# The pooled branch and the merge gates of the second block, computed inside its attention and parked in DRAM

## The chip, the cores and the metric

The kernel runs on one core of one Trainium2 chip. The time is device microseconds of that core, from one launch of the whole program; the time given is the median of several executions.

## The reference

Two transformer blocks are applied to 512 tokens of 1024 features, in float32. The first has latent attention beside a retention branch, and a layer of 16,384 experts. The change lies in the mixer of the second block:

```python
h = rms_norm(x, norm_mix)
u, q, kc, vc, ksl, vsl, kwn, vwn, g_nsa, g_merge = split(h @ w_in)
y_pool = pool_mixer(u, w_pool, pool_scale)   # means over the last 2, 4, 8, 16 tokens less the token, times w_pool
y_nsa = nsa_mixer(q, kc, ..., g_nsa)         # 16 heads, 2 groups: compressed, selected and window keys
g_a, g_b = split(sigmoid(g_merge))
merged = g_a * (y_pool @ w_proj_pool) + g_b * (y_nsa @ w_proj_nsa)
x = x + merged @ w_out
```

After it come a norm, a feed-forward layer of 4096 hidden features, and the last norm. `y_pool`, `g_a` and `g_b` need `h` alone; only `y_nsa @ w_proj_nsa` needs the attention.

## The kernel before

**Arithmetic.** Arrays are kept as [feature, token]: tiles of 128 features on the partitions and 512 tokens along them. A product in float32 is made of three passes over operands that are split into a high and a low part (`hi` is the value rounded to float32r, `lo` the rest). `fm` (L249) multiplies 128 columns of a weight with all 512 tokens: 24 matmuls of 512 columns where the input has 1024 features (3 passes of 8 tiles), 12 where it has 512. `weights` loads one chunk of weights by a DMA on SyncE's queue (L222, 512 KB for 1024 features), rounds it on ScalarE (L210, tile `wh`) and subtracts on VectorE or GpSimd (L211, tile `wl`); the engine of the subtraction alternates from chunk to chunk. There are two buffers each for the raw chunk, `wh` and `wl`.

**The second block's mixer**, in the order of the code. The normed input `hn` (tiles `h2h`, `h2l` in the profile) is made; the keys and values of the three kinds follow. Then for each of two groups `g`: `queries(g)` makes the group's queries (four chunks `w_q`, each rotated in `rope_fm`, which passes it through a DMA on ScalarE's queue), and `attend(i, g, c, ...)` is called for four tiles `i` of 128 queries and two sets `c` of four heads, eight times a group. One `attend` makes the scores (PE, L1401 and L1402), adds the mask and takes the maximum (VectorE, L1431), the exponential (ScalarE, L1436), the compressed keys' softmax (`cs`, with GpSimd at L1441, L1444, L1449), scales by gate over sum (L1457 on VectorE, L1455 on GpSimd for one head of four), transposes (PE, L1469, copied out at L1471) and multiplies with the values (PE, L1474, into the one PSUM bank of the kind `o`). The result is split into `ynh` and `ynl`.

After both groups come the pooled branch (four chunks `w_u`, shifted sums on VectorE and GpSimd, L1491 to L1507; a product with `w_pool`, L1516, into `yps`) and the merge: for each of eight chunks `c` of 128 output features a gate `y` (`gate`, weights `w_gm`), the attention's projection (`gated`, `w_pn`, 24 matmuls), a gate `x` (`w_gm`), the pooled projection (`w_pp`, 12 matmuls), and `merged`, which adds the two:

```python
def gate(name, c, x):
    w = wfm(name, c)
    ps = mmps()
    fm(ps, w, hn, 0, 0, T)
    S.activation(x, ps, AF.Tanh, scale=0.5)
    return x
...
    V.scalar_tensor_tensor(x, x, 1.0, ps, op0=OP.add, op1=OP.mult)
...
for c in range(KD):
    y = gate("w_gm", KD + c, two(t2)[:, :T])
    gated("w_pn", c, ysl, KD, y)
    x = gate("w_gm", c, two(t2)[:, :T])
    gated("w_pp", c, yp, 4, x)
    merged(x, y, mg, c)
```

`residual` then multiplies with `w_out2` and adds to the residual stream `h1`, which stays in SBUF all the while, in the two halves of the kind `xb`.

**Who sets the order.** Here the instructions are not placed by hand. A scheduler orders them when the program is compiled: each engine, and SyncE's queue of DMAs, gets one fixed order, in which the instructions that come first in the code go first among those that the scheduler holds to be ready. On the chip each engine runs its own order strictly. Tiles are handed out from pools: the kind `t2` of this block has five buffers of 2 KB a partition (queries' rotation, shifted sums and gates share it), PSUM has two banks of the kind `mm`, which all products with weights share.

Of the kernel before, what the change touches and what calls it, by code (L numbers as in the profile page):

```python
# [9 lines left out]
F32 = mybir.dt.float32  # L10
# [8 lines left out]
T = 512          # tokens whose outputs are wanted  # L19
M = 16           # meta tokens; in the key order they come after the tokens  # L20
# [31 lines left out]
def _constants():  # L52
# [5 lines left out]
    tri01 = (q[None, :] >= q[:, None]).astype(f)                       # [m, c]  # L58
# [47 lines left out]
def _layout(i):  # L106
    i = {k: np.asarray(v) for k, v in i.items()}
    a = _constants()
    h = np.concatenate([i["x"][0], i["meta_tokens"]], 0)               # [528, 1024]
# [36 lines left out]
    pe = np.stack([i["pe_k_2"][0], i["pe_v_2"][0]], 0)                  # [2, 32, 64]  # L146
    pe = pe.transpose(2, 0, 1).reshape(64, 64)
    a["pe"] = np.ascontiguousarray(np.concatenate([pe, pe], 0))          # [(g dh), (k/v, l)]
    a["w_c1"] = np.stack([i[n][0].reshape(2, 16, 64, 256).transpose(0, 2, 1, 3).reshape(P, 16 * 256)  # half, dh, l, hidden
# [16 lines left out]
# ---------------------------------------------------------------- the program  # L166
def build(tc, A, OUT):
# [29 lines left out]
    # constants  # L197
# [10 lines left out]
    def split(src, hi, lo, lo_eng=None):  # L208
        """hi is src rounded to float32r, lo the rest."""
        S.copy(hi, src)  # L210
        (lo_eng or V).tensor_tensor(lo, src, hi.bitcast(F32), op=OP.subtract)  # L211
# [6 lines left out]
    def weights(ap, n, lo_pool=3, tag="w"):  # L218
        """One chunk of weights from DRAM, split in two float32r parts."""
# [14 lines left out]
    def wfm(name, c, kt=KD, width=P, c0=0):  # L234
        """some columns of weights, by tiles of features"""
        n = kt * width
        return kview(weights(A[name][c][:, c0:c0 + n], n, 2), kt, width)
# [7 lines left out]
    def fm(out, w, act, c0, t0, n, kt=KD, hooks=()):  # L245
        """out [128 columns of w, n tokens]; hooks: what comes after the first, the second pass"""
# [7 lines left out]
    def tm(out, w, act, c0, n, t0, m, kt=KD):  # L254
        """out [m tokens, n columns of w]"""
# [8 lines left out]
    def rstd_cols(sqs, n, width, out, first=0, after=None):  # L264
        """out[token, tile] = 1 / sqrt(mean over the features + eps) of the tokens from first up to n; sqs(t0, m):
        the squares of m tokens, [feature, token]; after: a factor of the tokens that comes first, and into out."""
# [17 lines left out]
    def ks(t):  # L284
        """the tiles [128, tokens] of t [128, k, tokens]"""
        return [t[:, k] for k in range(t.shape[1])]
# [3 lines left out]
    class Squares:  # L290
        """sum of the squares of the tiles [128 features, n tokens] of the residual stream, as they come"""
# [3 lines left out]
        def add(self, x, eng=None, a=0, b=None, last=False):  # L295
            """the last tile's squares stay by themselves"""
# [12 lines left out]
    class Norm:  # L309
        """RMS norm over the features (partitions and tiles) of the tiles src, some tokens after the others;  # L310
        put(k, tile, a, b): tokens a .. b of a normed tile."""
        def __init__(self, src, sqs, g0, put, pieces=HALVES, dst=None):
# [3 lines left out]
            S.activation(self.col[:, 7:8], eps, AF.Sqrt)    # (its table is in place when the norm needs it)  # L316
            self.rowt = two(sqs.tp, "row")

        def cols(self, i):
            """1 / sqrt(mean + eps) of each token"""  # L320
# [3 lines left out]
        def row(self, i):  # L324
            """the same, along the partitions"""
# [31 lines left out]
    def by_halves(act, jobs, hooks=()):  # L357
        """products of act with columns of weights, jobs: (weights, first column, done(ps, a, b)); all jobs for
        half of the tokens, then for the other; hooks: what comes within the first product"""
# [7 lines left out]
    def residual(get, act, sqs=None, norm=None):  # L367
        """adds act's product with the weights get(k) (and their first column) to the residual stream; the last
        tiles by halves of the tokens, with the first half's norm among the products of the second"""
# [20 lines left out]
    def rope_op(dst, src, c, sn, sp, shape, tp, add=None):  # L390
        """dst = rotation of src, both [m, heads, 2 * half]; c, sn, sp: cos, -sin, sin"""
# [15 lines left out]
    def rope_tab(rope, off, w, m, h):  # L407
        """views of a packed table [cos | cos | -sin | sin], the same for each head"""
# [9 lines left out]
    def two(tp, name="t2", dt=F32):  # L418
        """a tile of 2 KB a partition, of a kind shared by many short lives"""
        return tp.tile([P, L], dt, name=name, tag="t2")  # L420

    # halves of arrays [feature, token]: the residual stream, and the experts' inputs
# [6 lines left out]
    hd = dp.tile([KD, P, T], F32, name="hd")                # the residual stream, while the experts run  # L429
# [3 lines left out]
    # ================================================================ first block: mixer  # L433
# [24 lines left out]
    # the latents come from the tokens before their norm, which goes into the latents' own: y = h gain / rms(h), and  # L458
    # rms of a latent c of y is sqrt(r^2 mean(c'^2) + eps), r = 1 / rms(h), c' = the latent of h gain
# [20 lines left out]
    # latent queries and keys, [feature, token], gained but not yet normed  # L480
# [27 lines left out]
    # shared rotary key, [token, 32]  # L508
# [25 lines left out]
    # four heads at a time: queries [96, head, token], their norm in the scale of the scores; keys  # L534
    # [96, head, (meta, token)]; values [token, head, 64]
# [4 lines left out]
    # the values of the meta tokens, one block of rows and columns per head  # L540
# [66 lines left out]
    # ---- retention: the decay since the start of the sequence is in the rotations' tables  # L607
    xh, qz = halves("rq", "xa")                             # queries of a head, zeros for the pair's other head
# [3 lines left out]
    kf = half_slot("rkf")                                   # keys [two heads' 64, pair, token]  # L612
    ktm = half_slot("rkt")[:, :, :T]                        # keys [token, tile (the last: meta), head's 64]

    def fm_pieces(w, pieces):
        """128 columns of w, [column, token]"""
# [7 lines left out]
    def ret_rope(x, j, n):  # L624
        """rotation of two heads [2 x 64, n tokens], the terms of a sum"""
# [35 lines left out]
    for j in range(2):                                      # meta tokens' probabilities of four heads, zero elsewhere  # L661
# [6 lines left out]
    def mla_attend(i, c):  # L668
        """a tile of queries, four heads"""
        n, t0 = (i + 1) * P, i * P  # L670
        mx = tp.tile([P, 3, 4], F32, name="mx", bufs=2)     # max, max of meta, -scaled max
# [944 lines left out]
```

## Time and profile before

| what | time |
|---|---|
| median of 3 executions | 2801.38 us (2801.16 to 2807.91) |
| the profiled execution, its span | 2800.6 us |
| second block's attention | 2010 to 2222 us |
| merge | 2222 to 2372 us |

The profiled execution's own time is its span; the median lies 0.8 us above it. Times inside the run are counted from the span's start. PE is TensorE's matmuls, PEld its weight loads (a weight load stands ahead of every matmul, so a wait of PE often shows as one of PEld), DVE is VectorE, ACT ScalarE, POOL GpSimd, SPq SyncE's queue of DMAs. Matmuls are pipelined, so a stretch in which PE is busy throughout need not run at its highest rate.

### The profile page before, as it was taken

To read this page: it belongs to the slowest core of one execution; us is meant where nothing else is said; L and a number is where in the kernel's file an instruction comes from. 1 tells how busy PE (TensorE), PEld (TensorE's weight loads), DVE (VectorE), ACT (ScalarE), POOL (GpSimd) and SP (SyncE) were. 2 spreads that over 40 slices of the span, in tenths; PEclk is the share of its full clock that TensorE was granted. 3 is DMA by queue.
4 is the path that set the end of the run, shared out by engine and by line. 5 is a ranking of instruction groups with operands and counts; after the bars stand their busy time and mean duration, and the time that the engine had idled before them with its cause. 6 is when DMAs were issued, how large, how long until landed. Compare 5 with 4: busy or idle time off the path is not lost.

```text
span 2800.6 us, 37220 instructions
## 1 busy us (share of the span) xinstructions
PE 2628.7 (94%) x13809; PEld 2246.1 (80%) x13809; DVE 1794.0 (64%) x3334; ACT 1131.5 (40%) x2064; POOL 1196.4 (43%) x831
## 2 busy tenths in 40 slices
PE   7889999998889799999999999998999999999998
PEld 6668778898789788888888888887666687878886
DVE  5673442259899736888988988896698521533333
ACT  4462343243777533333333333333566422422322
POOL 2322132325455926666666666662333333211111
PEclk9999999999999899999999999998999999999998
DMA  3312123322345467888888888884210132222221
GB/s 112 101 54 83 65 72 127 114 85 96 121 142 170 128 228 281 305 313 321 316 310 305 314 319 300 299 285 147 81 37 20 38 98 98 105 84 104 92 93 58
DMA packets 166149, 449.67 MB, mean 161 GB/s; under 512 B 14544, under 2 KB 67152, under 8 KB 159312
## 3 DMA queue, kind: packets, MB, share of 16 engines
q1 hardware_dynamic: 125648, 308.31, 32.0%
q0 software_dynamic: 36864, 134.23, 14.1%
q10 hardware_dynamic: 3456, 4.76, 0.7%
q8 instruction: 108, 1.77, 0.2%
q14 instruction: 73, 0.60, 0.1%
HBM read 413.10 MB, written 29.36 MB: 158 GB/s over the span
## 4 chain that ended last, share of the span: by engine, by line
PE 33%; DVE 22%; issue 9%; DMA 5%; POOL 4%; ACT 3%; ACTq 0%; DVEq 0%; SPq 0%; POOLq 0%
PE mm L249 21%; DVE vl L211 4%; PE py L1144 4%; PE pu L249 3%; DVE oh L1063 3%; DVE yg L958 2%; DVE row L948 2%; DMA row<-in_u_rows_dram,eg 2%; DMA row<-in_v_rows_dram,eg 2%; POOL oh L1038 1%; DVE al L211 1%; ACT ah L210 1%; PE tp L1469 1%; DVE act L1134 1%; PE o L1474 1%
## 5 line engine op out<-in xcount | busy, mean ns | idle before, releaser
L211 POOL TENSOR_TENSOR wl<-wr,wh 128x1024 fp32r<-128x1024 f32 (+1 forms) x199 | 480.7, 2416 | 572.6 <-ACT wh L210 277.2
L210 ACT CAST wh<-wr 128x1024 fp32r<-128x1024 f32 (+2 forms) x271 | 275.1, 1015 | 326.7 <-PE mm L249 213.3
L249 PE MATMUL pu<-xf,wh 128*128 128x384 f32 x2048 | 398.2, 345 | 0.4 <-ACT wh L210 0.4
L249 PEld LDWEIGHTS pu<-xf,wh 128*128 128x128 f32 x2048 | 366.2, 192 | 7.5 <-ACT wh L210 0.6
L210 ACT CAST ah<-act 128x384 fp32r<-128x384 f32 x128 | 65.9, 515 | 484.9 <-DVE act L1134 484.9
L211 DVE TENSOR_TENSOR al<-act,ah 128x384 fp32r<-128x384 f32 x128 | 201.7, 1576 | 79.6 <-ACT ah L210 78.3
L943 POOL DMA_INDIRECT row<-in_v_rows_dram,eg x128 | 193.6, 1512 | 132.6 <-DVE yg L958 101.5
L943 POOL DMA_INDIRECT row<-in_u_rows_dram,eg x128 | 185.4, 1449 | 130.8 <-DVE row L948 108.2
L1144 PE MATMUL py<-vh,ah 128*128 128x512 f32 x768 | 201.7, 397 | 26.7 <-ACT ah L210 26.6
L249 PE MATMUL pu<-xf,wl 128*128 128x384 f32 x1024 | 207.1, 344 | 5.3 <-POOL wl L211 5.3
L211 DVE TENSOR_TENSOR vl<-vr,vh 128x1024 fp32r<-128x1024 f32 x128 | 172.7, 1349 | 52.4 <-ACT vh L210 52.4
L1144 PE MATMUL py<-vl,ah 128*128 128x512 f32 x768 | 198.8, 394 | 0.0
L1144 PE MATMUL py<-vh,al 128*128 128x512 f32 x768 | 196.5, 390 | 0.0
L1144 PEld LDWEIGHTS py<-vh,ah 128*128 128x128 f32 x768 | 142.2, 189 | 60.3 <-ACT ah L210 37.7
L249 PEld LDWEIGHTS pu<-xf,wl 128*128 128x128 f32 x1024 | 184.4, 192 | 6.3 <-POOL wl L211 6.3
L958 DVE SCALAR_TENSOR_TENSOR yg<-row,ag,yg 128x1024 f32<-128x1024 f32 x127 | 167.9, 1322 | 16.4 <-DMA row<-in_v_rows_dram,eg 14.3
L948 DVE SCALAR_TENSOR_TENSOR row<-row,xg 128x1024 f32<-128x1024 f32 x128 | 168.4, 1346 | 10.8 <-DMA row<-in_u_rows_dram,eg 10.6
L1144 PEld LDWEIGHTS py<-vl,ah 128*128 128x128 f32 x768 | 146.2, 190 | 31.2
L1144 PEld LDWEIGHTS py<-vh,al 128*128 128x128 f32 x768 | 145.2, 189 | 30.4
L210 ACT CAST vh<-vr 128x1024 fp32r<-128x1024 f32 x128 | 134.3, 1049 | 78.8 <-DMA vr<-in_v_rows_dram 42.3
L1063 DVE TENSOR_TENSOR oh<-iota,eT 128x1024 f32<-128x1024 f32 x96 | 150.5, 1589 | 18.0 <-PE mm L1072 17.6
L211 POOL TENSOR_TENSOR wwl<-wwr,wwh 128x2048 fp32r<-128x2048 f32 x10 | 45.9, 4594 | 266.4 <-ACT wwh L210 266.4
(461 smaller groups left out, 5253.8 us busy)
## 6 DMA issues: line engine op xcount, KB each, us to landing
wr<-in_u_T_dram SPq DMA_DIRECT2D x128, 512.0 KB
vr<-in_v_rows_dram SPq DMA_DIRECT2D x128, 512.0 KB
wwr<-in_w_f_dram SPq DMA_DIRECT2D x32, 1024.0 KB
gates<-stg SPq DMA_DIRECT2D x24, 1024.0 KB
gin<-gates SPq DMA_DIRECT2D x16, 1536.0 KB
wr<-in_w_gm_dram SPq DMA_DIRECT2D x16, 512.0 KB
wr<-in_w_rv_dram SPq DMA_DIRECT2D x8, 512.0 KB
wr<-in_w_rg_dram SPq DMA_DIRECT2D x8, 512.0 KB
```

The lines of the kernel that those rows point to most:

```text
L210: S.copy(hi, src)
L211: (lo_eng or V).tensor_tensor(lo, src, hi.bitcast(F32), op=OP.subtract)
L249: TE.matmul(out, w[a][k][:, c0:c0 + P], act[b][k][:, t0:t0 + n], start=i == 0 and k == 0, stop=i == 2 and k == kt - 1)
L943: G.indirect_dma_start(out=r, out_offset=None, in_=src, in_offset=bass.IndirectOffsetOnAxis(ap=eg[:, k:k + 1], axis=0))
L948: V.scalar_tensor_tensor(r, r, 1.0, xg, op0=OP.mult, op1=OP.mult, accum_out=ag[:, k:k + 1])
L958: V.scalar_tensor_tensor(yg[0], r, ag[:, k:k + 1], yg[0], op0=OP.mult, op1=OP.add)
L1038: G.tensor_tensor(ov[:, h], ov[:, h], iv[:, 4 * c + h, None].to_broadcast([P, 16, 16]), op=OP.mult)
L1063: V.tensor_tensor(a1, iota[:, None, None, :].to_broadcast([P, 2, 4, P]), eT[:, :2, b0 + q0:b0 + q0 + 4, None].to_broadcast([P, 2, 4, P]), ...
L1134: V.tensor_tensor(av, av, gated_acts.g[:, :, (e % NE) * TB:(e % NE + 1) * TB], op=OP.mult)
L1144: TE.matmul(py[2 * t + d], x[:, t * P:(t + 1) * P], w[:, d * 512:(d + 1) * 512], start=e == 0 and i == 0, stop=e == P - 1 and i == 2)
L1469: TE.transpose(pt[:, x * P:(x + 1) * P], sts[a][br][:, j * P:(j + 1) * P], ident)
L1474: TE.matmul(po[b * 64:b * 64 + 64, :2 * P], vt[:, j, br, g], pT[:, b * 256:b * 256 + 256], start=False, stop=last, skip_group_check=True)
```

## The change

The pooled branch, all 16 gates and the eight pooled projections become a generator, `beside`, whose 29 steps are called between the calls of `attend`: 15 places in each group, after `attend` of the tile `i` 1, 2, 2 or 3 of them, one fewer after the second set of tile 1. The finished gates `y` and the finished products `x` are stored to DRAM (`merge`), 256 KB each, and loaded again in the merge, which keeps only `w_pn` and the sum. Since `yps` now needs a place during the attention, the residual stream is stored to DRAM (`hd2`) right after the first products of the block, `yps` takes its place (the kind `xb`), and `h1` is loaded back after the attention. `yp` products use the PSUM kind `mm`, no longer `s`. `gate`, `gated` and `merged` are not changed.

```diff
+    hd2 = dp.tile([KD, P, T], F32, name="hd2")
+    merge = [dp.tile([KD, P, T], F32, name=n) for n in ("mgx", "mgy")]
...
     by_halves(hn, [(wkc[x], 0, kc_done(x)) for x in range(2)], norm.hooks(1))
+
+    for k in range(KD):
+        nc.sync.dma_start(hd2[k], h1[k][:, :T])
...
+    yp = tuple(ks(h[:, :, :T]) for h in halves("yps", "xb", F32R)[0])
+
+    def beside():
+        pooled = []
+        for g in range(4):
+            w = wfm("w_u", g)
+            ps = mmps()
+            fm(ps, w, hn, 0, 0, T)
...
+            V.tensor_tensor(d[:, :16], d[:, :16], u[:, :16], op=OP.subtract)
+            yield
+        wpl = two(t2)[:, :T]
+        nc.sync.dma_start(wpl, A["w_pool"])
+        for g, d in enumerate(pooled):
+            ps = mmps("yp")
+            TE.matmul(ps, wpl[:, g * P:(g + 1) * P], d, start=True, stop=True)
...
+        yield
+        for c in range(KD):
+            y = gate("w_gm", KD + c, two(t2)[:, :T])
+            nc.sync.dma_start(merge[1][c], y)
+            yield
+            x = gate("w_gm", c, two(t2)[:, :T])
+            yield
+            gated("w_pp", c, yp, 4, x)
+            nc.sync.dma_start(merge[0][c], x)
+            yield
+
+    side = beside()
     for g in range(2):
         Q = queries(g)
         yh, yl = half_slot("ynh", F32R), half_slot("ynl", F32R)
         for i in range(NT):
             for c in range(2):
                 attend(i, g, c, Q, yh, yl)
+                for _ in range((1, 2, 2, 3)[i] - (i == c == 1)):
+                    next(side, None)
         ysl[0].extend(ks(yh))
         ysl[1].extend(ks(yl))
...
-    yps = pool("pooled", stack=st).tile([P, KD, T], F32R, name="yps")
...
+    h1 = [x for x in halves("h1", "xb")[1]]
+    for k in range(KD):
+        nc.sync.dma_start(h1[k][:, :T], hd2[k])
+    mp = pool("parked", bufs=8, stack=st)
...
     for c in range(KD):
-        y = gate("w_gm", KD + c, two(t2)[:, :T])
+        x, y = (mp.tile([P, T], F32, name="park") for _ in range(2))
+        nc.sync.dma_start(x, merge[0][c])
+        nc.sync.dma_start(y, merge[1][c])
         gated("w_pn", c, ysl, KD, y)
-        x = gate("w_gm", c, two(t2)[:, :T])
-        gated("w_pp", c, yp, 4, x)
         merged(x, y, mg, c)
```

## Rows read from the trace of the kernel before

**Rows 1.** The page's head and its busy time by engine, whole run.
```profile
span 2800.6 us, 37220 instructions
...
PE 2628.7 (94%) x13809; PEld 2246.1 (80%) x13809; DVE 1794.0 (64%) x3334; ACT 1131.5 (40%) x2064; POOL 1196.4 (43%) x831
```

**Rows 2.** Chosen stretches: length, busy time and count by engine, clock, DMA.
```profile
2010.00:2222.00 212.00, 200.92 (x1187) 137.06 (x1186) 179.43 (x610) 133.85 (x375) 71.56 (x100) 0.98 0.10 31
2222.00:2340.00 118.00, 118.00 (x516) 96.67 (x515) 24.41 (x33) 34.37 (x43) 42.08 (x18) 1.00 0.29 94
2340.00:2372.00 32.00, 30.32 (x132) 24.48 (x132) 6.58 (x9) 8.96 (x11) 11.61 (x5) 1.00 0.32 107
...
1000.00:1500.00 500.00, 490.73 (x2384) 435.19 (x2385) 405.10 (x482) 174.12 (x239) 307.64 (x182) 0.99 0.84 298
```

**Rows 3.** Three pieces of 20 us out of the attention, the same columns.
```profile
2010.00:2030.00 20.00, 16.96 (x90) 12.10 (x88) 17.98 (x82) 14.30 (x54) 8.61 (x13) 0.96 0.17 57
...
2090.00:2110.00 20.00, 16.62 (x106) 10.80 (x104) 18.70 (x50) 11.89 (x29) 8.50 (x9) 1.00 0.03 8
2110.00:2130.00 20.00, 19.77 (x133) 13.63 (x134) 15.41 (x85) 13.87 (x50) 4.53 (x10) 0.91 0.06 20
```

**Rows 4.** The chain that ended last, about the attention's end: start, length, what.
```profile
2186.45 3.60 DVE s L1457 x5
...
2221.03 145.37 PE mm L249 x634
```

**Rows 5.** Waits of PE's weight loads in the attention: total us, times, longest.
```profile
PEld tp L1469 <- issue: 16.5, 42, 0.8
PEld tp L1469 <- DVE s L1457: 15.4, 19, 3.1
PEld o L1474 <- ACT pT L1471: 6.8, 22, 0.9
...
PEld tp L1460 <- POOL cs L1449: 3.0, 8, 0.5
PEld o L1474 <- DVE pT L1471: 2.9, 10, 0.4
```

**Rows 6.** Timeline of PE in the attention: start, length (us), engine, line.
```profile
2114.17 0.64 PE L249 MATMUL mm<-h2l,wh 128*128 128x512 f32 x2
2114.74 1.08 PE L1474 MATMUL o<-pT,vt 128*64 128x256 f32 x8
```

**Rows 7.** Timeline of SyncE's DMA issues through the attention.
```profile
2022.78 62.04 SPq L222 DMA_DIRECT2D wr<-in_w_u_dram  x4
2108.63 0.33 SPq L222 DMA_DIRECT2D wr<-in_w_gm_dram  x1
...
2192.69 0.33 SPq L222 DMA_DIRECT2D wr<-in_w_pp_dram  x1
2194.21 0.33 SPq L1513 DMA_DIRECT2D t<-in_w_pool_dram  x1
```

**Rows 8.** VectorE's groups in the merge, 2222 to 2372 us.
```profile
L839 DVE SCALAR_TENSOR_TENSOR t<-t,mm 128x512 f32<-128x512 f32 x16 | 11.0, 688 | 103.1 <-PE mm L249 103.1
L211 DVE TENSOR_TENSOR wl<-wr,wh 128x1024 fp32r<-128x1024 f32 x8 | 9.7, 1219 | 0.0
...
L211 DVE TENSOR_TENSOR wl<-wr,wh 128x512 fp32r<-128x512 f32 x8 | 5.5, 685 | 0.0
```

**Rows 9.** ScalarE's table loads and gates within the attention.
```profile
L1436 ACT ACT_TABLE_LOAD x1 | 1.3, 1283 | 0.0
L831 ACT ACTIVATE t<-mm 128x512 f32<-128x512 f32 x2 | 1.2, 602 | 0.7 <-PE mm L249 0.7
```

**Rows 10.** The scaling at L1457, ns min/median/max.
```profile
L1457 DVE TENSOR_SCALAR s<-s,sm x96: 273/436/2566, 2017.6 to 2206.2; 128x128 f32<-128x128 f32 x24, 128x256 f32<-128x256 f32 x24, 128x384 f32<-128x384 f32 x24, 128x512 f32<-128x512 f32 x24
```

**Rows 11.** GpSimd's halves of weights within the attention.
```profile
L211 POOL TENSOR_TENSOR wl<-wr,wh 128x1024 fp32r<-128x1024 f32 x5 | 12.0, 2402 | 9.9 <-issue 9.8
```

**Rows 12.** An earlier store of the residual stream, issue time in ns.
```profile
L888 SPq DMA_DIRECT2D hd<-h x8: 326/327/330, 525.5 to 565.4; - x8
```

More of the change, by code (lines that the diff above doesn't have):

```diff
@@ L1477, in attend @@
         split(pv, yh[:, 2 * c:2 * c + 2, t0:t0 + P], yl[:, 2 * c:2 * c + 2, t0:t0 + P])
+    yp = tuple(ks(h[:, :, :T]) for h in halves("yps", "xb", F32R)[0])
[5 more added lines that the diff above has]
+            fm(ps, w, hn, 0, 0, T)
+            u = two(t2)[:, :T]
+            S.copy(u, ps)
+            cur = u
+            for e in range(g + 1):
+                sft = 1 << e
+                nx = two(t2)[:, :T]
+                G.tensor_copy(nx[:, :sft], cur[:, :sft])
+                V.tensor_tensor(nx[:, sft:], cur[:, sft:], cur[:, :T - sft], op=OP.add)
+                cur = nx
+            d = gp.tile([P, T], F32, name="pooled", bufs=4)
+            pooled.append(d)
+            V.scalar_tensor_tensor(d[:, 16:], cur[:, 16:], 1.0 / (2 << g), u[:, 16:], op0=OP.mult, op1=OP.subtract)
+            V.tensor_tensor(d[:, :16], cur[:, :16], cst2[:, K_INV + 16 * g:K_INV + 16 * g + 16], op=OP.mult)
+            V.tensor_tensor(d[:, :16], d[:, :16], u[:, :16], op=OP.subtract)
[5 more added lines that the diff above has]
+            TE.matmul(ps, wpl[:, g * P:(g + 1) * P], d, start=True, stop=True)
+            gg_ = gcol[:, G_POOL + g:G_POOL + g + 1]
+            S.activation(yp[0][g], ps, AF.Copy, scale=gg_)
+            V.scalar_tensor_tensor(yp[1][g], ps, gg_, yp[0][g].bitcast(F32), op0=OP.mult, op1=OP.subtract)
+        yield
[9 more added lines that the diff above has]
+    side = beside()
     for g in range(2):
@@ L1484, in build @@
                 attend(i, g, c, Q, yh, yl)
+                for _ in range((1, 2, 2, 3)[i] - (i == c == 1)):
+                    next(side, None)
         ysl[0].extend(ks(yh))
         ysl[1].extend(ks(yl))
-    pooled = []
-    for g in range(4):
-        w = wfm("w_u", g)
-        ps = mmps()
-        fm(ps, w, hn, 0, 0, T)
-        u = two(t2)[:, :T]
-        S.copy(u, ps)
-        cur = u
-        for e in range(g + 1):
-            sft = 1 << e
-            nx = two(t2)[:, :T]
-            G.tensor_copy(nx[:, :sft], cur[:, :sft])
-            V.tensor_tensor(nx[:, sft:], cur[:, sft:], cur[:, :T - sft], op=OP.add)
-            cur = nx
-        d = gp.tile([P, T], F32, name="pooled", bufs=4)
-        pooled.append(d)
-        V.scalar_tensor_tensor(d[:, 16:], cur[:, 16:], 1.0 / (2 << g), u[:, 16:], op0=OP.mult, op1=OP.subtract)
-        V.tensor_tensor(d[:, :16], cur[:, :16], cst2[:, K_INV + 16 * g:K_INV + 16 * g + 16], op=OP.mult)
-        V.tensor_tensor(d[:, :16], d[:, :16], u[:, :16], op=OP.subtract)
+    for _ in side:
+        pass
     sta.close()
     stk2.close()
-    yps = pool("pooled", stack=st).tile([P, KD, T], F32R, name="yps")
-    yp = (ks(yps[:, :4]), ks(yps[:, 4:]))
-    wpl = two(t2)[:, :T]
-    nc.sync.dma_start(wpl, A["w_pool"])
-    for g, d in enumerate(pooled):
-        ps = bank("s", "yp")
-        TE.matmul(ps, wpl[:, g * P:(g + 1) * P], d, start=True, stop=True)
-        gg_ = gcol[:, G_POOL + g:G_POOL + g + 1]
-        S.activation(yp[0][g], ps, AF.Copy, scale=gg_)
-        V.scalar_tensor_tensor(yp[1][g], ps, gg_, yp[0][g].bitcast(F32), op0=OP.mult, op1=OP.subtract)
+    h1 = [x for x in halves("h1", "xb")[1]]
+    for k in range(KD):
+        nc.sync.dma_start(h1[k][:, :T], hd2[k])
+    mp = pool("parked", bufs=8, stack=st)
     qst = ExitStack()
```

## The prediction

> **What bounds the kernel now.** I read the page first, for the whole run: TensorE is busy 94% of the span [rows 1], so a gain has to come out of time in which it stands still or runs below its rate. The stretches show where that is. In the merge TensorE is busy 148.3 of 150 us while VectorE needs 31; in the attention before it TensorE is busy 200.9 of 212 us and VectorE 179.4 [rows 2]. The chain of work that ended last says the same: from 2221 us it is one unbroken piece of 634 products, 145.37 us long, while inside the attention it passes again and again through VectorE, as in the 3.60 us of five scalings [rows 4]. So the merge is pure TensorE work at full rate, 145.37 / 634 = 0.229 us a matmul of 512 columns, with three other engines at rest; the attention is a mixture in which TensorE now and then waits for VectorE.
>
> How much it waits is the one thing that this change can win, because no matmul is saved. By busy time TensorE is idle 212 - 200.9 = 11.1 us there [rows 2], most of it in two places: 3.0 us in 2010:2030 and 3.4 us in 2090:2110, where VectorE is busy 18 to 18.7 of 20 us; in 2110:2130 it is 0.2 us [rows 3]. Busy time hides short waits, so I also read the waits of its weight loads: for results of VectorE, ScalarE and GpSimd 15.4 + 6.8 + 3.0 + 2.9 = 28.1 us, and another 16.5 us in which a transposition's load waits for nothing that the profile shows [rows 5]. The 28.1 us are the ceiling: other products could run there. The 16.5 us come 42 times at about 0.4 us, ahead of transpositions; I take them for turns between kinds of matmul, which more products do not remove.
>
> **What moves.** 16 gates of 24 matmuls and 8 pooled projections of 12, 480 matmuls, 480 x 0.229 = 110 us of TensorE, go from the merge in between the attention's steps. The merge keeps 8 x 24 = 192, 44 us. Taken alone that is nothing won: the 110 us lengthen the attention. The gain is what they fill of the 28.1 us. Two ends: none (the products that the scheduler already mixes in have not removed these waits) and all. For the idle time proper, 11.1 us, I count 9 as filled: in 2010:2030 and 2090:2110 it is VectorE that is late, and with 110 us more of TensorE's work over the same VectorE work it will be less loaded (below). Of the other 28.1 - 11.1 = 17 us, short waits inside a step, I take half. **Gain 18 us**, between 0 and 28.
>
> **What that costs the other engines.** On VectorE go half of the 24 subtractions of weights (4 + 4 at 1.219 us, 4 at 0.685) and 8 products with the gate at 0.688 us [rows 8]: 12.5 + 5.5 = 18 us. Its 179 us become 197 in a stretch of 212 + 110 - 18 = 304 us, less what of the merge ran there already: 65% where it was 85%. So VectorE's share is hidden under TensorE; were it not, those 18 us would cancel the gain. ScalarE has 133.9 of 212 us now, and at most the merge's 43.3 come to it [rows 2]; 177 of 304 is no bound. A change of tables could have been the trap, tanh among exponentials: but there was one table load in the attention, though two gates ran among its exponentials [rows 9], so 14 more cost none. Both are taken at nothing.
>
> **Turns.** A run of products against a product with the values costs something extra: two L249 matmuls begin at 2114.17 and the next kind at 2114.74, 0.57 us where 2 x 0.229 = 0.46 would do: 0.11 us [rows 6]. If a chunk is cut into about four runs, 24 chunks make 100 runs; some 40 of them beside such a product cost 4 us. None is the low end, all of them on both sides, 200 x 0.11 = 22 us, the high one. **Cost 4 us.** By the Trainium skill (TensorEngine Tiling (Array Packing), Key Properties) a change of the tiling mode drains the array, and the products with the values use half of its columns; by that rule the price goes with the number of changes, and if every run paid at both ends the sum would come out 18 us higher than mine. That the turn above took 0.11 us agrees with it.
>
> **The stores and loads.** The store of the residual stream is 8 issues of 0.33 us [rows 12] and 2.1 MB. At the rate that the experts' stage reaches, 298 GB/s [rows 2], that is 7 us of transfer, at a time when only weights are loaded: nothing, at worst 7 us if the first weights of the keys queue behind it. 16 stores of 256 KB in the attention, at 31 GB/s there now [rows 2], are nothing. In the merge 8 x 512 KB of weights, 16 loads of 256 KB and the 2.1 MB of `h1` come together: 10.5 MB in 44 us, 238 GB/s, below 298, so it fits. But `h1` lies where `yps` lay and cannot be loaded before the last pooled projection is done, and what stands behind it on SyncE's queue waits too: the third chunk of `w_pn` onward (two are held by buffers) and parked tiles. Two chunks are 11 us of TensorE, the 2.1 MB 7 us and the chunk itself 1.8: nearly hidden. **Cost 2 us**, 0 to 10.
>
> **Sum.** -18 + 4 + 2 = -12: 2800.6 - 12 = 2788.6 by the profiled execution, and with the median 0.8 us above its span **2789 us**.
>
> **Rivals.**
> *Nothing is filled.* The order is not that of the code: a `w_pp` chunk was loaded before `w_pool`, which stands ahead of it in the code, and all of `w_u` and the first gate were loaded during the attention [rows 7]. So the scheduler already fills what it takes for idle, and what remains may be lateness that it does not foresee, or be bound by buffers (five `t2`, two chunks). The gain is 0 to 6, the costs 6: 2795 to 2807, say 2801. Against it: in 62 us only four chunks were issued [rows 7], so the filling was thin, and the new places bring it forward.
> *GpSimd holds VectorE: slower.* Twelve more subtractions go to GpSimd, 8 at 2.4 us [rows 11] and 4 at half. The scaling at L1457 has a median of 0.44 us, but one took 2.57 us [rows 10], the length of such a subtraction. If each of the twelve catches a scaling, 8 x 2.1 + 4 x 0.9 = 20 us of lateness fall on the step that TensorE waits longest for [rows 5]. With 12 of these 20 on the path the gain is gone; with all, and the waits not filled, it is 2801 + 6 + 20 - 9 = 2818; from 21 us on the path it is slower than can be told from no change even with my gain. For it: L1457 is on the chain [rows 4]. Against: five such subtractions ran there already, and the median is unmoved. The Trainium skill (SBUF — State Buffer, Who interferes with whom) states that the two engines share a port pair as an exclusive lock for a whole instruction; the 2.57 us agree with it, and by it each catch costs the full length.
> *More is filled.* All 28 us and fewer turns: 2801 - 28 + 2 = 2775.
>
> **Chances.** My forecast 0.53; nothing filled 0.27; VectorE held up, or the merge starved at its start, 0.12; more 0.08. A measurement of this kernel tells about 0.3%, 8.4 us, from no change. Most of the forecast (2781 to 2793) and the last case count as faster: 0.57. Nothing filled, and the forecast's weak end: 0.29 the same; slower 0.14. The range reaches from all filled, 2774, into the slower case, 2809.
>
> **What would show it.** Right: PE's waits for L1457 and L1471 shrink in sum though the stretch is some 290 us; VectorE's share falls to about two thirds; no long gap at the group change, though `queries(1)` now has 15 steps ahead of it; the merge is 44 us without holes. Wrong: L1457 of 2 us or more in number beside GpSimd's `wl`; PE waiting for `wh` or `wl` at the start of the merge with `h1`'s loads just ahead; or steps of `beside` left over behind the last `attend`, which would mean that they filled nothing.

## The result, and the profile after

The changed kernel takes 2826.9 us (median of 4 executions, 2822.75 to 2829.04); the kernel before took 2804.64 us (2801.16 to 2809.89, 4 executions) beside it. The ratio is 1.0078, with an interval from 1.0061 to 1.0094: slower by about 22 us, where 12 us of gain were forecast.

The page of the changed kernel, head and busy time by engine (against [rows 1]):

```profile
span 2827.1 us, 37288 instructions
...
PE 2636.4 (93%) x13809; PEld 2246.2 (79%) x13809; DVE 1810.2 (64%) x3334; ACT 1130.0 (40%) x2064; POOL 1191.1 (42%) x831
```

The number of matmuls is the same. The two profiled spans differ by 26.5 us, of which PE's busy time explains 7.7; the rest is idle time of PE. Where it lies can be read off two products in PE's timeline: the first product of the second block's scores and the first one with `m2h`, which opens `w_out2`. In the kernel after they are:

```profile
2004.74 0.30 PE L1406 MATMUL s<-KH,q 128*128 128x288 f32 x1
...
2391.84 0.86 PE L249 MATMUL mm<-m2h,wh 128*128 128x512 f32 x3
```

That is 387.1 us for attention and merge, where the same two products of the kernel before stand 364.2 us apart. So 22.9 of the 26.5 us lie between them. From there to the end of the run it is 434 and 435 us, and from the normed input to the first score 80 us in both; the other 2.7 us of the difference arose ahead of what was changed.

The stretches of the changed kernel (length, then busy time and count of PE, PEld, DVE, ACT and POOL, granted clock, DMA share, GB/s), against [rows 2, 3]:

```profile
2012.00:2348.00 336.00, 307.68 (x1626) 218.76 (x1625) 210.99 (x634) 163.69 (x413) 95.14 (x111) 0.98 0.21 64
2348.00:2392.00 44.00, 44.00 (x196) 35.90 (x195) 14.02 (x18) 13.39 (x17) 20.32 (x11) 1.00 0.64 214
2120.00:2140.00 20.00, 16.98 (x103) 11.01 (x102) 10.35 (x14) 7.73 (x15) 5.47 (x4) 1.00 0.14 45
```

The merge is what was forecast: 44 us, PE busy throughout. The attention is not. PE stands still for 28.3 us of it, where it was 11.1, although VectorE's share has fallen to 63%. What PE's weight loads wait for in the attention, 2004.5 to 2349.1 us (total us, times, longest), against [rows 5]:

```profile
PEld tp L1474 <- DVE s L1462: 19.7, 16, 3.3
PEld tp L1474 <- issue: 18.1, 45, 0.8
PEld tp L1465 <- POOL cs L1454: 10.5, 15, 2.3
...
PEld o L1479 <- ACT pT L1476: 9.4, 34, 0.4
...
PEld o L1479 <- DVE pT L1476: 4.2, 12, 0.4
```

(L1462 is the scaling that was L1457; L1465 the transposition of `cs`, before L1460; L1474, L1476 and L1479 the transpositions, their copies and the products with the values.) None of these waits got shorter. The scalings' rose from 15.4 to 19.7 us, and the wait for `cs`, whose three small steps are GpSimd's, from 3.0 to 10.5.

Pieces of the chain that ended last (start, length, what), against [rows 4]:

```profile
2035.30 1.36 issue
2036.66 2.40 POOL wl L211
2039.06 0.60 POOL cs L1449
2040.12 0.71 POOL t L1500
2040.83 0.48 POOL cs L1454
2041.35 0.33 PE tp L1465
...
2121.95 5.88 DVE s L1462 x5
2127.87 0.55 PE tp L1474 x3
...
2349.39 42.63 PE mm L249 x187
```

The reader is to see GpSimd at 2036: a subtraction of a step's weights, and then, in its queue, `cs` of the attend, the copy of the pooled sums (L1500) and `cs` again, until PE can transpose. At 2121 it is the chain of one `attend`: five scalings, then its transpositions. Three subtractions on GpSimd are on the chain within the attention (2.40, 2.42 and 2.41 us); none was before.

The timeline at the second place shows who is held by whom:

```profile
2121.95 6.26 DVE L1462 TENSOR_SCALAR s<-s,sm 128x512 f32<-128x512 f32 x6
...
2122.66 2.40 POOL L1460 TENSOR_TENSOR s<-s,sm 128x512 f32<-128x512 f32 x2
...
2123.18 1.88 PE L249 MATMUL mm<-yps,wh 128*128 128x512 f32 x7
...
2125.02 2.52 POOL L211 TENSOR_TENSOR wl<-wr,wh 128x1024 fp32r<-128x1024 f32 x1
...
2127.87 0.55 PE L1474 MATMUL tp<-cstt,s 128*128 128x128 f32 x3 [2.81 <-DVE s L1462]
```

PE got seven products of a step, and then its order has transpositions whose scalings come 2.81 us late. Why they are late shows in the six scalings taken singly (least, median and longest in ns):

```profile
L1462 DVE TENSOR_SCALAR s<-s,sm x6: 473/940/2557, 2122.0 to 2127.7; 128x512 f32<-128x512 f32 x6
```

Two lasted 1.26 us, each beside one of GpSimd's two scalings. The fifth began at 2125.26, 0.24 us after the subtraction of a step's weights (L211), and lasted 2.56 us. The sixth, with GpSimd at rest, took 0.47. The same stands at the attention's end:

```profile
2332.59 2.52 POOL L211 TENSOR_TENSOR wl<-wr,wh 128x1024 fp32r<-128x1024 f32 x1
...
2335.45 0.90 PE L1474 MATMUL tp<-cstt,s 128*128 128x128 f32 x3 [2.83 <-DVE s L1462]
```

It stood once in the kernel before too, where this wait makes up most of the 3.4 us of idle time in 2090:2110 [rows 3]:

```profile
2106.07 2.52 POOL L211 TENSOR_TENSOR wl<-wr,wh 128x1024 fp32r<-128x1024 f32 x1
...
2109.33 0.55 PE L1469 MATMUL tp<-cstt,s 128*128 128x128 f32 x3 [2.67 <-DVE s L1457]
```

Another kind of place is GpSimd's queue at 2098 us of the changed kernel: the last operand of `cs` was ready at 2098.37 us, but a subtraction was running.

```profile
2098.30 2.42 POOL L211 TENSOR_TENSOR wl<-wr,wh 128x1024 fp32r<-128x1024 f32 x1 [19.40 <-ACT wh L210]
...
2100.68 0.40 POOL L1446 TENSOR_TENSOR cs<-cs,mc 128x128 f32<-128x128 f32 x1
```

### The profile page after: what moved, and what is told of

It reads as the page before. It is cut to its first block, busy times and chain, and to the rows that moved or that the text cites. A ratio compares the mean times of both kernels' runs of the same rounds, so it can differ in the third digit from the quotient of the medians.

```text
span 2827.1 us, 37288 instructions
## 1 busy us (share of the span) xinstructions
PE 2636.4 (93%) x13809; PEld 2246.2 (79%) x13809; DVE 1810.2 (64%) x3334; ACT 1130.0 (40%) x2064; POOL 1191.1 (42%) x831
## 4 chain that ended last, share of the span: by engine, by line
PE 31%; DVE 20%; issue 10%; DMA 6%; POOL 6%; ACT 3%; ACTq 0%; DVEq 0%; POOLq 0%; SPq 0%
PE mm L249 19%; DVE vl L211 4%; PE pu L249 3%; DMA row<-in_u_rows_dram,eg 3%; PE py L1146 3%; DVE row L950 3%; DVE oh L1065 2%; DMA row<-in_v_rows_dram,eg 2%; DVE yg L960 2%; PE o L1479 2%; POOL oh L1040 1%; POOL wl L211 1%; PE tp L1474 1%; POOL row L945 1%; DVE s L1462 1%
## 5 line engine op out<-in xcount | busy, mean ns | idle before, releaser
L211 POOL TENSOR_TENSOR wl<-wr,wh 128x1024 fp32r<-128x1024 f32 (+1 forms) x199 | 476.5, 2395 | 596.8 <-ACT wh L210 309.9
L249 PE MATMUL pu<-xf,wh 128*128 128x384 f32 x2048 | 399.7, 346 | 0.4 <-ACT wh L210 0.4
L249 PEld LDWEIGHTS pu<-xf,wh 128*128 128x128 f32 x2048 | 367.6, 193 | 7.6 <-ACT wh L210 0.6
L211 DVE TENSOR_TENSOR al<-act,ah 128x384 fp32r<-128x384 f32 x128 | 204.7, 1599 | 79.3 <-ACT ah L210 78.0
L249 PE MATMUL pu<-xf,wl 128*128 128x384 f32 x1024 | 207.2, 344 | 5.3 <-POOL wl L211 5.3
L211 DVE TENSOR_TENSOR vl<-vr,vh 128x1024 fp32r<-128x1024 f32 x128 | 161.5, 1262 | 52.2 <-ACT vh L210 52.2
L249 PEld LDWEIGHTS pu<-xf,wl 128*128 128x128 f32 x1024 | 184.5, 192 | 6.3 <-POOL wl L211 6.3
L960 DVE SCALAR_TENSOR_TENSOR yg<-row,ag,yg 128x1024 f32<-128x1024 f32 x127 | 176.1, 1387 | 16.9 <-DMA row<-in_v_rows_dram,eg 14.7
L211 DVE TENSOR_TENSOR wl<-wr,wh 128x1024 fp32r<-128x1024 f32 (+3 forms) x72 | 85.6, 1189 | 119.5 <-PE mm L249 81.6
```

The costliest lines, as they stand in the source:

```text
L249: TE.matmul(out, w[a][k][:, c0:c0 + P], act[b][k][:, t0:t0 + n], start=i == 0 and k == 0, stop=i == 2 and k == kt - 1)
L960: V.scalar_tensor_tensor(yg[0], r, ag[:, k:k + 1], yg[0], op0=OP.mult, op1=OP.add)
```

## The experiments

The same 22 us could have several owners. Order, parking and GpSimd were named ahead of the first four runs (steps behind the attention, inside the attend, no subtraction on GpSimd, next scores first); after these, GpSimd's part was divided into queue and port, and the bank was added. **Order**: the steps stand between the calls of `attend`, the scheduler follows the code's order among what is ready, and so neighbouring attends no longer overlap. From the timeline I took the time by which the first maximum of an attend lies ahead of the previous one's last product with the values: 8.6 to 21.1 us at all 15 borders before, 216 us in sum; after only 70 us, and at seven borders a gap instead, 28 us long at the change of groups. **Queue**: GpSimd has both the attends' small steps and eleven more subtractions of weights (16 in place of 5, twelve of them of about 2.4 us), and they wait for each other. **Port**: the prediction's rival, subtractions that hold up VectorE's scalings. **Bank**: the pooled product takes the PSUM kind `mm`, which all products with weights share. **Parking**: the stores, loads and the residual stream through DRAM.

Ratios below are to the kernel before, with 95% intervals. "Mixer" is the distance between the two products above (364.2 us before, 387.1 after). It comes from the one profiled execution of a run, which took between 3.4 us less and 6.1 us more than the median of that run; a difference of some 6 us between two mixers settles nothing by itself.

**The steps behind the attention.** All 29 steps come after the last `attend`; parking and everything else stays.

```diff
                 attend(i, g, c, Q, yh, yl)
-                for _ in range((1, 2, 2, 3)[i] - (i == c == 1)):
-                    next(side, None)
```

> All 29 steps stand behind the last attend in the code; the parking in DRAM, the reload of the residual stream and the new place of the pooled product stay. Theory 'order' (a step stands ahead of the next attend in the code, so its products run before the next scores, the attends no longer overlap and VectorE stands idle): the attends overlap again as in the kernel before, attention about 212 us, total within 6 us of the kernel before (ratio 0.998 to 1.003). Theory 'parking' (the stores, reloads and the queue behind them cost the time): stays slower, ratio 1.005 to 1.010. Theory 'GpSimd' (its extra subtractions hold VectorE among the attends): also near the kernel before, since the subtractions leave the attention; this run does not tell it from 'order'.

Measured: 1.0031 [1.0019, 1.0044], at the upper end of what 'order' had said (1.003); mixer 372.2 us (in an execution of 2821.3 us, where the median is 2815.2). Some 60% of the loss needs the steps among the attends, 40% does not. The attends overlap as they did before (215 us). What is left shows at the attention's end, in the chain and in a stretch of this run:

```profile
2221.10 1.90 PE tp L1474 x8
2223.00 1.69 PE yp L1513 x2
2224.68 1.01 PE o L1479 x8
```

```profile
2210.00:2230.00 20.00, 16.73 (x82) 9.12 (x80) 11.09 (x23) 8.07 (x17) 2.76 (x3) 0.83 0.00 1
2233.00:2386.00 153.00, 153.00 (x669) 125.16 (x668) 31.61 (x38) 44.11 (x56) 44.65 (x23) 1.00 0.48 163
```

No product with weights stands between the attend's last pieces; the pooled product `yp` does; PE is idle for 3.3 us of these 20, and the granted clock is 0.83. After it, the merge with all parking runs 153 us without a hole.

**The pooled product in its old banks.** The run above, with one line more:

```diff
-            ps = mmps("yp")
+            ps = bank("s", "yp")
```

> All steps behind the attention, as before, and the pooled product back in the PSUM banks of the scores, where the kernel before has it. Theory 'bank' (waiting for the late pooled sums, it holds both banks of the products with weights, so no gate can cover the attention's end; 8 us in the run with all steps at the end): the gates cover the end again, ratio 0.998 to 1.001. Parking (the 8 us are the stores and reloads): ratio stays at 1.002 to 1.004.

Measured: 1.0012 [1.0002, 1.0021], mixer 363.8 us, between what 'bank' (up to 1.001) and parking (from 1.002) had said. The stretches about the attention's end in this run:

```profile
2200.00:2222.00 22.00, 20.69 (x124) 11.95 (x122) 13.45 (x31) 11.69 (x25) 3.18 (x4) 1.00 0.04 12
2222.00:2370.00 148.00, 148.00 (x647) 120.85 (x647) 30.72 (x38) 42.55 (x55) 44.22 (x23) 1.00 0.49 167
```

The attention is 215.9 us, as before, and the merge is dense. So part of the first run's loss was the bank: some 5 us by the ratios (0.0019 x 2804), whose intervals just overlap, and 8 us by the mixers, of which the first comes from an execution 6 us above its run's median. Everything that is parked costs about 3 us (0.0012 x 2804; 0.6 to 5.9 by the interval), of which the mixer shows nothing.

**The steps inside the attend**, between its scalings and its transpositions, where the code would have them cover the wait for the scalings.

```diff
+        yield
         po = bank("o", "o")
...
-                attend(i, g, c, Q, yh, yl)
+                a = attend(i, g, c, Q, yh, yl)
+                next(a)
                 for _ in range((1, 2, 2, 3)[i] - (i == c == 1)):
                     next(side, None)
+                next(a, None)
```

> The same steps at the same attends, but between an attend's scaling and its transpositions, instead of behind them: scores, steps, transpositions and values. Order: the steps now cover the softmax of their own attend and the next scores follow the values at once; the gaps between attends shrink, 10 to 25 us faster than the changed kernel (ratio to the kernel before 0.999 to 1.004). GpSimd and parking: nothing of theirs is changed, ratio 1.006 to 1.010.

Measured: 1.0048 [1.0032, 1.0065], mixer 377.5 us. That lies between what 'order' (up to 1.004) and the others (from 1.006) had said, and decides for neither. PE's weight loads waited for scalings and `cs` 9.5 us in place of 30.2, but for the copies `pT` 21.4 in place of 13.8. A wait that is covered at one place of the attend turns up at the next.

**No subtraction of a step on GpSimd.** VectorE makes all `wl` of the steps.

```diff
-        return kview(weights(A[name][c][:, c0:c0 + n], n, 2), kt, width)
+        return kview(weights(A[name][c][:, c0:c0 + n], n, lo_of[0]), kt, width)
...
+                lo_of[0] = V
                 for _ in range((1, 2, 2, 3)[i] - (i == c == 1)):
                     next(side, None)
+                lo_of[0] = 2
```

> The steps' subtractions of weights all on VectorE, none on GpSimd; all else as in the changed kernel. GpSimd: the waits of TensorE for the scaling and for the compressed keys shrink, 10 us or more won (ratio 1.000 to 1.004). Order: VectorE has idle time enough for 16 us more, 0 to 4 us either way (ratio 1.006 to 1.010).

Measured: 1.0034 [1.0022, 1.0047], mixer 371.3 us. Some 12 us come back, although the attends overlap as little as in the changed kernel (66 us); 'order' had said 0 to 4, 'GpSimd' 10 or more. GpSimd is a cause.

**Fifteen steps behind each group.**

```diff
-                for _ in range((1, 2, 2, 3)[i] - (i == c == 1)):
-                    next(side, None)
         ysl[0].extend(ks(yh))
         ysl[1].extend(ks(yl))
+        for _ in range(15):
+            next(side, None)
```

> The steps in two lumps of 15, behind the last attend of each group. Order: within a group the attends overlap as in the kernel before, only the boundary between the groups pays; with what the steps behind the attention still cost (8 us when all of them stand there), 5 to 12 us over the kernel before (ratio 1.002 to 1.005). Were the cost one per step, wherever it stands, the ratio would stay at 1.006 to 1.010.

Measured: 1.0035 [1.0022, 1.0049], as 'order' had said (1.002 to 1.005), mixer 372.9 us. A gap of 65 us opens between the groups' attends, and PE is busy all through it (the stretch of this run):

```profile
2120.00:2190.00 70.00, 69.99 (x325) 55.37 (x322) 14.64 (x18) 21.71 (x30) 16.96 (x9) 1.00 0.36 115
```

So a gap between attends is no loss in itself. It costs only where no products fill it.

**The next attend's scores ahead of the steps.** In the code now: scores of the next attend, steps, values of the last one.

```diff
-                attend(i, g, c, Q, yh, yl)
+                a = attend(i, g, c, Q, yh, yl)
+                next(a)
                 for _ in range((1, 2, 2, 3)[i] - (i == c == 1)):
                     next(side, None)
+                if late:
+                    next(late.pop(), None)
+                late.append(a)
```

> Each attend's scores and softmax stand ahead of the steps, and the transpositions and values of the attend before it behind them: scores of k+1, steps, values of k. Order: the overlap of neighbouring attends is written into the code, so this is the fastest of the variants with steps among the attends, faster than the kernel before by 5 to 20 us (ratio 0.993 to 0.998), with VectorE no longer idle at the boundaries. GpSimd and parking: ratio 1.005 or more.

Measured: 1.0020 [1.0011, 1.0030], mixer 370.0 us. The overlap is 321 us, more than before, and PE waits for scalings and `cs` only 2.8 us; still some 6 us are missing by the ratio and by the mixer, and both expectations are missed (0.993 to 0.998 for 'order', 1.005 or more for the others). PE's idle time is 15.3 us in the attention of this run, the first of these lines. A third of it lies in two stretches, the pooled sums and the attention's end:

```profile
2000.00:2328.60 328.60, 313.33 (x1670) 226.81 (x1668) 212.28 (x663) 167.60 (x420) 97.27 (x112) 0.99 0.23 78
2040.00:2060.00 20.00, 18.06 (x86) 11.58 (x86) 17.68 (x69) 11.13 (x33) 4.35 (x8) 0.91 0.12 41
2310.00:2328.00 18.00, 14.89 (x97) 8.39 (x95) 7.64 (x16) 7.30 (x17) 2.99 (x3) 1.00 0.44 167
```

In most of the first the steps have nothing but the pooled product, which waits for VectorE's sums; at the second no steps are left.

**The attends off GpSimd.** The changed kernel, where the attends' `cs` steps and the fourth head's scaling go to VectorE and the steps' subtractions stay.

```diff
-        G.tensor_tensor(cs, cs, mc[:, :, None].to_broadcast([P, 4, 32]), op=OP.subtract)
+        V.tensor_tensor(cs, cs, mc[:, :, None].to_broadcast([P, 4, 32]), op=OP.subtract)
...
-                    G.tensor_tensor(s, s, r.to_broadcast([P, n]), op=OP.mult)
+                    V.tensor_scalar(s, s, r, None, op0=OP.mult)
```

(the other two `cs` steps likewise)

> The changed kernel with the attends' own work on GpSimd (the three steps of the compressed keys, the fourth head's scaling) on VectorE; the weights' subtractions stay on GpSimd as they were. Theory 'queue' (an attend's small steps stand behind a subtraction of 2.4 us in GpSimd's order): nothing of an attend is in that order any more, 8 to 15 us won over the changed kernel (ratio 1.002 to 1.005), though VectorE has 30 us more to do. Theory 'port' (GpSimd's subtractions hold VectorE's instructions up, whoever else uses GpSimd): no gain, or a loss (ratio 1.007 to 1.014).

Measured: 1.0005 [0.9996, 1.0015], mixer 364.2 us: 20 of the 22 us are back by moving 80 small instructions onto VectorE, the engine that I had taken for the late one. 'Port' fails as the main cause, since the subtractions stayed; 'queue' had the right sign, but had said 8 to 15 us. The stretch of this run, and then PE's waits in it:

```profile
2012.00:2326.00 314.00, 300.92 (x1634) 218.77 (x1633) 213.18 (x715) 162.00 (x413) 45.39 (x31) 1.00 0.23 74
```

```profile
PEld tp L1474 <- issue: 15.8, 41, 0.4
PEld o L1479 <- ACT pT L1476: 7.7, 25, 0.8
PEld o L1479 <- DVE pT L1476: 7.1, 17, 1.1
PEld tp L1474 <- DVE s L1462: 3.6, 6, 2.2
```

The scalings' wait is 3.6 us, PE's idle time 13.1 us. The overlap of the attends, though, is only 81 us, and the gap at the change of groups is still 27 us. So lost overlap by itself does not make the kernel slower.

**The same edit in the kernel before**, as a control.

> The kernel before, with the attends' three small steps of the compressed branch and the fourth head's scaling on VectorE instead of GpSimd; a control for the same edit in the changed kernel. 'Queue' (these steps are late only behind the subtractions of weights, of which five ran beside the attention before): the ratio is 1.000, between 0.998 and 1.002. 'The edit is good by itself' (VectorE does these steps faster wherever they stand, and the changed kernel only got the same gift): it wins some 20 us here as well, 0.993. 'Port': VectorE has 12 more us of work at 85% load, so it loses, 1.002 to 1.004.

Measured: 1.0002 [0.9993, 1.0011], as 'queue' had said; mixer 368.9 us (in an execution of 2812.1 us, where the median is 2806.8). The edit is no gift by itself. It pays only where the steps' subtractions run among the attends; the two uses of GpSimd together are what costs.

**The attends off GpSimd, and the pooled product in the scores' banks** (both edits shown above, in the changed kernel).

> The changed kernel with the attends off GpSimd, and the pooled product in the banks of the scores. 'Bank' as a cost of its own (8 us at the attention's end): 8 us off 1.0005, so 0.9975 to 0.9985. 'Bank only where the product stands at the end': amid the attention other products cover the wait, and the ratio stays at 1.0005, between 0.9995 and 1.0015. If the scores miss their banks meanwhile: over 1.002.

Measured: 0.9992 [0.9983, 1.0001], mixer 362.8 us. It lies between the two expectations, 3.6 us below the run without the banks (0.0013 x 2804), with intervals that just overlap. Whether the bank costs less amid the attention than the some 5 us at its end isn't settled.

**All together.** The next scores first, the steps' subtractions on VectorE, the pooled product after the first two gates, the last three steps kept for the attention's end.

```diff
+                lo_of[0] = V
-                for _ in range((1, 2, 2, 3)[i] - (i == c == 1)):
+                for _ in range(0 if g and i == 3 and c else (1, 2, 2, 3)[i] - (i == c == 1)):
                     next(side, None)
+                lo_of[0] = 2
...
             x = gate("w_gm", c, two(t2)[:, :T])
             yield
+            if c == 0:
+                wpl = two(t2)[:, :T]
...
+                yield
             gated("w_pp", c, yp, 4, x)
```

> Scores of k+1, steps, values of k; the steps' subtractions all on VectorE; the pooled product only after the first two gates; the last three steps behind the last attend. If order, GpSimd's queue and the bank are the causes, each of the three remedies counts: 5 to 15 us faster than the run with the next scores first, ratio 0.996 to 1.000. If it stays at 1.002, what is left is the turns of TensorE and no order of this kind wins.

Measured: 2800.34 us beside 2804.24, 0.9986 [0.9977, 0.9995], as expected (0.996 to 1.000), mixer 359.7 us. It is the only version here that is faster than the kernel before by more than its interval, and by some 4 us. PE's waits in its attention (lines shifted by 2 or 3):

```profile
PEld tp L1477 <- issue: 16.2, 42, 0.4
PEld o L1482 <- ACT pT L1479: 9.5, 29, 1.0
PEld o L1482 <- DVE pT L1479: 5.7, 13, 1.1
PEld o L1472 <- DVE pT L1470: 4.4, 11, 1.3
...
PEld tp L1477 <- DVE s L1464: 3.5, 4, 1.5
```

**All together, but the attends off GpSimd** in place of the subtractions.

> The kernel of all remedies together (next scores first, the pooled product after the first two gates, the last three steps behind the last attend), but GpSimd relieved the other way: the attends' small steps and fourth scaling go to VectorE, the steps' subtractions of weights stay on GpSimd. 'Queue': it does not matter which of the two leaves GpSimd, so the ratio is that of all together, 0.9986, give or take 0.001; somewhat better, 0.997, if the longer subtractions cost VectorE more than the small steps. 'Port' (the subtractions on GpSimd stop VectorE): it is slower than all together, 1.001 to 1.004.

Measured: 0.9994 [0.9985, 1.0003], mixer 362.8 us, as 'queue' said: which of the two leaves GpSimd matters little, and 'port' fails once more. The remedies don't add up: order alone won 16 us of the loss, GpSimd alone 12 or 20, both together, with the pooled product moved and three steps kept back, 24 to 26. They take away the same waits in part.

The waits of PE's weight loads side by side, each over the attention of its run (summed from the view of waits; us), with the attention's length and what is left of it without its L249 products at 145.37 / 634 = 0.2293 us each [rows 4]:

| run | ratio | scalings and `cs` | `pT` | attention | products | left |
|---|---|---|---|---|---|---|
| before | 1 | 18.4 | 10.1 | 215.9 | 222 | 165.0 |
| after | 1.0078 | 30.2 | 13.8 | 344.6 | 678 | 189.1 |
| no subtraction on GpSimd | 1.0034 | 20.9 | 15.4 | 328.9 | 678 | 173.4 |
| next scores first | 1.0020 | 2.8 | 20.1 | 328.6 | 684 | 171.8 |
| attends off GpSimd | 1.0005 | 6.8 | 17.7 | 322.8 | 684 | 166.0 |
| all together | 0.9986 | 4.4 | 19.6 | 318.3 | 684 | 161.5 |

The stretches behind the attention of before, after and all together, each from its own run; the second number is PE's busy time:

```profile
2001.80:2217.70 215.90, 204.21 (x1205) 139.53 (x1203) 184.48 (x639) 136.64 (x378) 73.08 (x101) 0.98 0.10 30
2004.50:2349.10 344.60, 315.79 (x1663) 224.76 (x1661) 218.13 (x663) 169.14 (x420) 96.44 (x112) 0.99 0.21 65
2006.80:2325.10 318.30, 309.73 (x1670) 225.46 (x1668) 216.29 (x674) 166.29 (x418) 72.94 (x100) 1.00 0.24 80
```

## Why the prediction was wrong

**Waits filled, -18 us: the step that failed.** It held that 110 us of products among the attends would fill 9 of 11.1 us of idle time and half of the short waits. In the changed kernel PE's idle time went from 11.1 to 28.3 us, and the attention without its products from 165.0 to 189.1 us. The products were there, but PE's order is fixed: at 2121 us seven of them ran, and then the transpositions stood ahead of the next ones and waited 2.81 us for scalings. I had treated products as something that flows into a hole wherever it opens. They fill only holes that the order foresaw. And I had put the idle time of 2090:2110 down to VectorE's load, which more products would thin out: 2.67 of its 3.4 us were a wait for one scaling that ran beside a subtraction on GpSimd, and the change puts more subtractions there. The three rivals, at 2775, 2801 and 2818 us, lie below the measured time as well.

The step was also too large without that failure. With the causes named above relieved, in the run of all together, 161.5 us are left in place of 165.0: 3.5 us won, not 18 (3.9 us by the ratio, 1.4 to 6.4 by its interval). The rest did not go away but moved: waits for scalings and `cs` fell from 18.4 to 4.4 us, those for `pT` rose from 10.1 to 19.6. Both sums together, 28.5 and 24.0, are the ceiling of which I had meant to fill 18. And PE's busy time without its products is 309.7 - 156.8 = 152.9 us there, 204.2 - 50.9 = 153.3 before: of the short waits inside a step, of which I took half, nothing shows as filled.

**GpSimd holds VectorE: the right engine, the right sign, a small part of the mechanism.** The rival was given 0.12 and 2818 us. It let each of twelve subtractions catch a scaling for its whole length. The scaling, min, median and max in ns, of the changed kernel, against [rows 10]:

```profile
L1462 DVE TENSOR_SCALAR s<-s,sm x96: 271/473/2560, 2020.3 to 2335.3; 128x128 f32<-128x128 f32 x24, 128x256 f32<-128x256 f32 x24, 128x384 f32<-128x384 f32 x24, 128x512 f32<-128x512 f32 x24
```

Two of 96 last over 2 us, where it was one, and all 96 together 59.1 us, where it was 54.3: 4.8 us in place of 20. The two are not without weight: PE's two longest waits for scalings, 2.81 and 2.83 us, come right behind them. By the Trainium skill (SBUF — State Buffer, Who interferes with whom), whichever of the two engines comes first keeps the ports that they share for its whole instruction; the catches of 2.56 us agree with it, but there are too few. The rival's sum also took 9 us off although it let the waits go unfilled; without that it reads 2801 + 6 + 20 = 2827, the measured time, but this would be luck, since its 20 us did not come about. What the runs show instead is that GpSimd's two tasks spoil each other: taking either of them away gives 12 or 20 us, while in the kernel before, taking the attends' small steps away gives nothing.

How those 20 us arise in single waits is only partly seen. The first `cs` step stood 2.3 us behind a subtraction in two of the 16 attends, three subtractions are on the chain (7.2 us), and PE's wait for `cs` rose by 7.5 us. Each edit also made the scheduler order PE's instructions anew, and no run held that order fixed. How much of the 20 us is waiting in GpSimd's queue, and how much a better order around a freer engine, stays open.

**Turns, +4.** Too high if anything. In the run of all together 462 products more were mixed in, and PE's busy time without products did not grow (152.9 against 153.3 us). Since the clock was lower before (0.98 against 1.00 over the attention; 3.4 us, last section), about as much may hide in that. In the changed kernel it did grow, by 7.0 us (315.8 - 155.5 = 160.3). Counted in PE's timeline, products with weights and products with the values adjoin there at 40 places, at 19 before, and at each the next matmul begins some 0.1 us later than it does without the change of kind (0.33 us behind a product with weights, where another such product begins 0.23 us behind it). By that estimate 21 more turns are 2 of the 7 us, and the lower clock is another 1.7 (5.1 less 3.4, last section); the rest is open.

**Stores and loads, +2.** Right as far as is shown: about 3 us (0.6 to 5.9) with the steps behind the attention, and no wait in the merge. **VectorE's 18 us, hidden.** Right: 63% where 65% was forecast. VectorE has time enough; it is late, not busy, and it could take the attends' small steps of GpSimd as well (213.2 us of busy time where it was 211.0, since its own 96 scalings took 38.7 us in place of 59.1). **ScalarE.** Nothing of it was seen as a bound.

**What was to show it.** The merge of 44 us without holes came. The waits for the scalings and for `pT` were to shrink and grew. The long gap at the group change was to be absent and came, 28 us; but the runs with a gap of 65 and of 27 us show that it costs nothing where products fill it. A part that the prediction did not have at all is the bank: it noted nothing of `yp` moving to `mm`, which cost some 5 us with the steps at the attention's end.

## What to carry to other kernels

Work that is off the busiest engine still passes through the side engines that the critical chain uses: before moving it next to a chain, list for each engine with an order of its own which small steps of the chain stand behind the newcomer's long ones, and move one of the two. Filling holes needs an order that has the filler exactly there; take for the gain only idle time that lies in long, foreseeable places, not a sum of short waits, which move down the chain when the first is covered. And a gap between stages is no loss until the stretch shows the bound engine idle in it.

## What was not expected of the hardware

Some holes in PE's work were followed by a lower granted clock. Two successive stretches of the changed kernel, at the attention's end:

```profile
2328.00:2336.00 8.00, 5.07 (x23) 3.63 (x22) 6.87 (x9) 3.60 (x7) 5.48 (x4) 0.92 0.00 0
2336.00:2344.00 8.00, 7.99 (x40) 4.68 (x38) 0.69 (x1) 2.18 (x4) 0.00 (x0) 0.65 0.67 199
```

PE was idle for 2.9 us of the first, and in the second, in which it was busy throughout, the clock was 0.65: part of it at the lower of the two levels (1.2 and 2.4 GHz). The same at 2048 to 2064 us, 0.93 and then 0.86. Over the attention the lost clock comes to (0.08 + 0.35 + 0.07 + 0.14) x 8 = 5.1 us of full rate, 3.4 us in the kernel before; in the runs of all together and of the attends off GpSimd no stretch of 8 us fell below 0.99. Such a hole is paid a second time. Not every hole is: of the five stretches of 8 us in which PE was idle for 2 us or more, the clock fell in or behind the two at 2048 and 2328 alone, and over 2120:2140, with the wait of 2.81 us, it stayed at 1.00.

A scaling of 128x512 on VectorE took 1.26 us beside one of 1.2 us on GpSimd, 2.56 us beside a subtraction of 2.5 us, and 0.47 us alone.
